# Grouped-query attention: the third converted block moves into its own job, and V is scaled instead of checked

## The chip, the cores and the metric

The kernel runs on one core of a Trainium2 chip. The metric is the device time of one execution in microseconds (us). Engines: PE (TensorE, matrix products), ACT (ScalarE, exponentials), DVE (VectorE, element by element), POOL (GpSimd, likewise, and issue of DMAs), SP (issue of DMAs). Each takes its instructions in order; they wait for each other by semaphores.

## The reference

```python
batch, seq, n_heads, n_kv_heads, dim = 8, 512, 32, 8, 64
scores = np.einsum('bhqd,bhkd->bhqk', Q, K_expanded) * (1 / np.sqrt(dim))
weights = np.exp(scores - np.max(scores, axis=-1, keepdims=True))
weights = weights / (np.sum(weights, axis=-1, keepdims=True) + 1e-10)
output = np.einsum('bhqk,bhkd->bhqd', weights, V_expanded)
```

Q, K and V are float32, four query heads share one head of K and V. The output is float32.

## The kernel before, in words

The maximum is not subtracted. The sums of the exponentials come out of the second product by a column of ones beside V, and each output is multiplied by the reciprocal of its sum. The sums (and V's largest value) are checked against bounds on the chip; where a bound is broken, a general path computes the result anew after the fast one.

Work is cut into 64 jobs, one for each batch and head of K: four query heads, in two pairs (`NPAIR`), of 512 queries against 512 keys. Scores are computed transposed, keys on partitions: a block is 128 keys by 512 queries, and a job has 16 of them: pair i, key chunk kc, head m of the pair. Two blocks that differ in m use different halves of PE's rows and are written next to each other as one pair of 128x1024. In `act_tile` PE writes such a pair to an `s_ps` tile of PSUM (two of these, two banks each) and ACT turns it into exponentials `pt` in 16 bits.

Not all blocks go to ACT. The first blocks of pair 1 are converted by DVE and POOL through bits of a 16-bit number: DVE scales the scores into an integer `u` (`exp_d`, L313); it masks its low bits, `f` (L325); POOL makes a factor `g` (L330) and a product `w` (L336); DVE adds `u` and `w` into `pt` one job later (`exp_d4`, L349). A narrow job takes two blocks so (jobs 0 to 3, those with j % 5 equal to 2, and the last two). A wide job (`WIDE`) takes three, which leaves ACT six pairs and one half, 128x512. The scores that DVE reads stand in `d_ps`, one tile of two banks, which also receives the transposed queries.

In a wide job j of before, the order by engine is: four ACT pairs, with the scores of DVE's first two blocks (`exp_d(j, 0, 2, ...)`) after the first; two groups of 16 products of the job before (`pv`, L377) between them; its reciprocal and scaling (`norm`, L417 and L422), which free the one pv tile; then a new `d_ps` tile whose second bank takes the score of ACT's lone half (`beside`), while the queries of job j + 2 are transposed into its first bank (L215). `apart` declares for ACT's reading and the transposes and copy that they touch different banks of the tile, since the recording layer otherwise orders users of one tile. DVE adds the previous job's `w` (L349), masks its own `u` (L325) and copies the queries (L220). In the last wide job of a round of five, the factor `g` is made on DVE after this copy. Next, the third block of job j + 1 is written alone to the second bank (`exp_d(j + 1, 2, 3, ...)`) and converted by DVE (L313, 128x512). The remaining two ACT pairs and 32 pv matmuls lie between.

V arrives by POOL's DMA queue and is converted to bf16 by it, straight into the tile `vt` with 65 columns for each head, the last of them ones. `check_v` reduces each quarter of it to its largest absolute value (L238); `check_sums` compares 128 reciprocals at a time with two bounds (L388).

The order is written by hand (`manual_schedule`); the recording layer adds the waits.

Of the kernel before, what the change touches and what calls it, by code (L numbers as in the profile page):

```python
# [33 lines left out]
SUM_LO = 64.0  # L34
SUM_HI = 57344.0
V_HI = 1.0e15
NLAST = 16
LAST_SUMS = NLAST * 2 * 4


WIDE = lambda j: 4 <= j < 62 and j % 5 != 2


# [24 lines left out]
def fast_path(ctx, tc, Q, K, V, out, flag, ident):  # L68
# [13 lines left out]
    const_pool = ctx.enter_context(tc.tile_pool(name="const", bufs=1))  # L82
    qnat_pool = ctx.enter_context(tc.tile_pool(name="qnat", bufs=4))
    knat_pool = ctx.enter_context(tc.tile_pool(name="knat", bufs=2))
    qt_pool = ctx.enter_context(tc.tile_pool(name="qt", bufs=3))
# [10 lines left out]

    ok = const_pool.tile([128, SPB * 2 * SC], FP32, name="ok")
    okv = const_pool.tile([128, B * SC], FP32, name="okv")
    okall = const_pool.tile([128, 1], FP32, name="okall")
# [4 lines left out]
    vt = [const_pool.tile([128, SC, KV, D + 1], BF16, name=f"v{j}") for j in range(2)]  # L104
# [4 lines left out]
    kn, qn, kt, qt, twice = {}, {}, {}, {}, {}  # L109

# [8 lines left out]

    def load_v(b, lo=0):  # L120
        to = vt[b % 2][:, :, lo:, 0:D]
        of = V[b, :, lo:, :].rearrange("(p sc) g d -> p sc g d", p=128)
        if lo:
            for sc in range(SC):
                nc.gpsimd.dma_start(out=to[:, sc], in_=of[:, sc])
        else:
            nc.gpsimd.dma_start(  # L127
                out=to.rearrange("p sc g d -> p (sc g) d"),
                in_=of.rearrange("p sc g d -> p (sc g) d"),
            )  # L130

# [103 lines left out]

    def check_v(b, sc):
        n = b * SC + sc
        nc.vector.tensor_reduce(  # L238
            out=okv[:, n:n + 1], in_=vt[b % 2][:, sc, :, 0:D], op=ALU.max, axis=AX.XY,
            apply_absolute_value=True,  # L240
        )

    NJOB = NU * 2
    DPAIR = NPAIR - 1

    def taken(j):
        return 3 if WIDE(j) else 2

# [3 lines left out]
    def act_tiles(j):  # L252
# [7 lines left out]

    CHECKS = {
        (j, at): divmod(n, SC) for n, (j, at) in enumerate(
            [(j, 0) for j in (3, 4, 6, 7, 8, 11, 12, 16, 17, 21, 22, 23, 26, 27, 31, 32)]
            + [(j, 0) for j in (36, 37, 38, 41, 42, 46, 47, 48, 51, 52, 56, 57, 60, 61, 62)]
            + [(62, 1)]
        )
    }

    KEYS = dict(zip((4, 10, 16, 26, 36, 41, 50), range(1, B)))
# [5 lines left out]
    LOADS = {1: [(load_q, 1, 0, 2 * HPG), (load_q, 1, 2 * HPG, 4 * HPG)]}  # L275
    in_jobs(load_k, 1, [3, 8, 12, 23, 32, 38, 48])
    in_jobs(load_q, 2, [3, 7, 8, 12, 17, 22, 23, 27, 32, 37, 38, 42, 47, 48])
    in_jobs(load_v, 1, [4, 13, 18, 28, 33, 43, 53])

# [15 lines left out]

    def act_tile(j, n, spare=None):
        group = act_tiles(j)[n]
        i, kc, lo = group[0]
        ps = s_pool.tile([128, 2, S], FP32, name="s_ps") if spare is None else spare
        for _, _, m in group:  # L300
            scores(j, ps[:, m, :], i, kc, m)
        return nc.scalar.activation(  # L302
            out=jobs[j]["pt"][:, i, kc, lo:, :], in_=ps[:, lo:, :], func=EXP, scale=scale
        )

    def exp_d(j, lo, hi, ps, other=None):
        st = jobs.setdefault(j, {})
        if "u" not in st:
            for name, dtype in (("u", I16), ("f", I16), ("g", BF16), ("w", BF16)):
                st[name] = dve_pool.tile([128, 3, S], dtype, name=name + "16")[:, 0:taken(j), :]  # L310
        for n in range(lo, hi):
            apart(scores(j, ps[:, n - lo, :], DPAIR, *divmod(d_block(j) + n, 2)), other)
        return lambda: nc.vector.tensor_scalar(  # L313
            out=st["u"][:, lo:hi, :], in0=ps[:, 0:hi - lo, :], scalar1=A_U, scalar2=B_U,
            op0=ALU.mult, op1=ALU.add,
        )

    def exp_d2(j, engine=None):  # L320
        st = jobs[j]
        by_bits = engine is None
        engine = engine or nc.gpsimd
        odd = j == NJOB - 2 or WIDE(j) and not WIDE(j + 1)
        nc.vector.tensor_single_scalar(  # L325
            out=st["f"], in_=st["u"], scalar=1023, op=ALU.bitwise_and
        )

        def factor():
            (nc.vector if odd else engine).tensor_scalar(  # L330
                out=st["g"], in0=st["f"], scalar1=-EXP_F1,
                scalar2=EXP_K * 2.0 ** (24 * by_bits), op0=ALU.add, op1=ALU.mult,
            )

        def product():
            engine.tensor_tensor(  # L336
                out=st["w"], in0=st["g"], in1=st["f"].bitcast(FP16) if by_bits else st["f"],
                op=ALU.mult,
            )
# [25 lines left out]
    def pv(j, i, lo, hi):  # L365
# [9 lines left out]
        for n in range(lo, hi):  # L375
# [3 lines left out]
                st["pt"][:, i, kc, m, qc * 128:(qc + 1) * 128],  # L379
                vt[b % 2][:, kc, 2 * gp + g, :],  # L380
# [4 lines left out]
    def in_bounds(outs, inv, first):  # L385
        ops = ((1.0 / SUM_HI, ALU.is_ge), (1.0 / SUM_LO, ALU.is_le))
        for out_, in1, (bound, op) in zip(outs, (first, outs[0]), ops):
            nc.vector.scalar_tensor_tensor(  # L388
                out=out_, in0=inv, scalar=bound, in1=in1, op0=op, op1=ALU.mult
            )  # L390


    full = []

    def check_sums():
        while full:
            flat = invs.pop(full.pop()).rearrange("p s m qc -> p (s m qc)")
            in_bounds((ok, ok), flat, ok)

    inv_last = const_pool.tile([128, NLAST, 2, SC], FP32, name="inv_last")  # L400

    def norm(j, i):
# [31 lines left out]
        if left > NLAST and n == SPB - 1:  # L434
            full.append(k)

    def all_checks():
        assert not full and not invs
        vmax = const_pool.tile([128, 1], FP32, name="vmax")
        nc.vector.tensor_reduce(out=vmax, in_=okv, op=ALU.max, axis=AX.X)  # L440
        okmin = const_pool.tile([128, 1], FP32, name="okmin")
        nc.vector.tensor_reduce(out=okmin, in_=ok, op=ALU.min, axis=AX.X)
        nc.gpsimd.tensor_scalar(
            out=okall, in0=vmax, scalar1=V_HI, scalar2=okmin, op0=ALU.is_le, op1=ALU.mult
        )

    LIMITS = ((1.0 / SUM_HI, ALU.is_ge), (1.0 / SUM_LO, ALU.is_le))
    rights = [const_pool.tile([128, LAST_SUMS], BF16, name=f"right{n}") for n in range(2)]

    def last_rights(lo, hi, first=None):  # L450
        inv = inv_last.rearrange("p s m qc -> p (s m qc)")
        for engine, right, (bound, op) in zip((first or nc.gpsimd, nc.gpsimd), rights, LIMITS):
            engine.tensor_scalar(
                out=right[:, lo:hi], in0=inv[:, lo:hi],
                scalar1=bound, scalar2=okall, op0=op, op1=ALU.mult,
            )
# [39 lines left out]
    for j in range(2):  # L496
        nc.gpsimd.memset(vt[j][:, :, :, D:D + 1], 1.0)
    load_k(0, 2, 4)
    load_k(0, 4, KV)
    load_q(0, 8, 16)  # L500
    load_v_head(0, 1)
    load_v(0, 2)
    nc.gpsimd.memset(ones, 1.0)
    nc.gpsimd.memset(ok, 1.0)

# [51 lines left out]
    two_keys(1)  # L557
    exp_d(0, 0, 2, d_tile())()
    act_tile(0, 3)
# [10 lines left out]
    for j in range(1, NJOB - 1):  # L570
# [8 lines left out]
        if j == 1:  # L579
            dma_k(0, 2)  # L580
        if j in KEYS:
# [6 lines left out]
        exp_d(j, 0, 2, d_tile())()  # L588
# [12 lines left out]
        bank = d_tile()  # L601
        beside = act_tile(j, 4, bank) if taken(j) > 2 else None

# [7 lines left out]
        rest = exp_d2(j)  # L611
        copies = [read() for read in reads]
        if rest:
            rest()
        if taken(j) == 2:
            act_tile(j, 4)
        pv(last, 1, 0, cut[0])
        act_tile(j, 5)
        if beside:
# [3 lines left out]
        if (j, 1) in CHECKS:  # L623
            check_v(*CHECKS[j, 1])
        if not beside:
            pv(last, 1, *cut)
        act_tile(j, 6)
        pv(last, 1, cut[1], 32)
# [5 lines left out]
    act_tile(j, 0)  # L634
    exp_d(j, 0, 2, d_tile())()
    all_checks()
# [139 lines left out]
```

## Time and profile before

| | |
|---|---|
| median of three runs | 404.75 us (404.59 to 404.81) |
| profiled execution, its own time | 404.57 us |
| its span in the profile | 402.8 us |
| busy share PE, DVE, ACT, POOL | 93%, 91%, 98%, 71% |
| ACT exponentials of 128x1024 | 400, 1122 ns each in the record |
| ACT exponentials of 128x512 from d_ps | 47, 724 ns each |
| DVE conversions of 128x512 | 47, 684 ns each |
| V checks | 32, 676 ns each |

The span runs from the first to the last recorded instruction; 1.8 us of the execution's time lie around it. A group's row gives line, engine, operation, output and input tiles, count, then busy time and mean length of one, then the idle time of the engine just before and what ended it. Lengths on ACT overlap: the next one starts before the last one's end, so the distance of ends gives the pace. In a timeline a row starts with its start and length in us; rows of equal instructions that follow each other are one row with a count.

### The profile page before, as it was taken

How to read it: one execution, taken by the hardware profiler on the slowest of the kernel's cores; microseconds unless marked ns; L12 is line 12 of the kernel's file. 1: busy time of each engine (PE TensorE's matmuls, PEld its weight loads, DVE VectorE, ACT ScalarE, POOL GpSimd, SP SyncE). 2: the span in 40 equal slices, each digit the busy share in tenths (PEclk: the TensorE clock that was granted, in tenths of full speed). 3: DMA queues.
4: the chain of work that ended last, by engine and by line, in shares of the span. 5: the costliest groups of instructions: out<-in, count | busy, mean ns of one | idle time of the engine just before them, and what ended most of it. 6: DMA issues, size and time to landing. Idle time of an engine off the chain costs nothing.

```text
span 402.8 us, 12997 instructions
## 1 busy us (share of the span) xinstructions
PE 375.8 (93%) x5670; PEld 228.0 (57%) x5670; DVE 366.4 (91%) x635; ACT 393.9 (98%) x454; POOL 286.8 (71%) x169
## 2 busy tenths in 40 slices
PE   7999999999999999999999999999999999999985
PEld 3565555555555555555555555555555555556554
DVE  4788998999999999999999999999999999999996
ACT  5999999999999999999999999999999999999995
POOL 9848577597587687687687686677776767765752
PEclk9999999999999999999999999999999999999999
DMA  9979999899999259999259999679369959222206
GB/s 145 163 190 182 91 288 225 164 211 237 184 214 206 107 88 247 192 239 182 107 84 226 168 227 197 208 109 252 110 170 202 175 169 128 107 106 106 88 34 201
DMA packets 82893, 67.73 MB, mean 168 GB/s; under 512 B 52752, under 2 KB 57872, under 8 KB 82832
## 3 DMA queue, kind: packets, MB, share of 16 engines
q0 software_dynamic: 45072, 24.91, 48.3%
q1 hardware_dynamic: 36688, 41.49, 36.6%
q8 instruction: 45, 0.74, 0.7%
q10 hardware_dynamic: 1072, 0.46, 0.4%
q14 instruction: 16, 0.13, 0.1%
HBM read 50.33 MB, written 33.55 MB: 208 GB/s over the span
## 4 chain that ended last, share of the span: by engine, by line
ACT 29%; PE 25%; POOL 24%; DVE 20%; issue 2%; ACTq 0%; DVEq 0%
ACT pt L302 28%; POOL w L336 16%; PE pv L377 12%; PE s_ps L284 9%; POOL g L330 8%; DVE pt L349 8%; DVE o_sb L422 4%; DVE f L325 4%; DVE qt L220 2%; PE d_ps L215 2%; DVE g L330 1%; DVE inv L417 1%; PE d_ps L284 1%; PE s_ps L510 1%; PE d_ps L377 0%
## 5 line engine op out<-in xcount | busy, mean ns | idle before, releaser
L302 ACT ACTIVATE pt<-s_ps 128x1024 f16<-128x1024 f32 x400 | 379.0, 1122 | 0.3 <-PE s_ps L284 0.2
L336 POOL TENSOR_TENSOR w<-g,f 128x1536 bf16<-128x1536 bf16 (+1 forms) x63 | 179.6, 2851 | 37.6 <-DVE g L330 33.4
L377 PEld LDWEIGHTS <-pt 128*128 128x128 f16 x4096 | 142.1, 98 | 81.2 <-issue 41.6
L377 PE MATMUL pv<-v,pt 128*128 128x65 bf16 x4032 | 177.8, 195 | 3.7 <-DVE o_sb L422 2.2
L284 PE MATMUL s_ps<-qt,kt 64*128 64x512 bf16 x746 | 152.3, 384 | 12.0 <-ACT pt L302 10.0
L330 POOL TENSOR_SCALAR g<-f 128x1536 bf16<-128x1536 int16 (+1 forms) x50 | 67.1, 1341 | 69.1 <-DVE f L325 69.0
L313 DVE TENSOR_SCALAR u<-d_ps 128x1024 int16<-128x1024 f32 (+1 forms) x111 | 109.9, 990 | 0.3
L284 PEld LDWEIGHTS <-kt 64*128 64x128 bf16 x960 | 50.2, 93 | 55.3 <-issue 31.5
L422 DVE TENSOR_TENSOR o_sb<-pv,inv 128x512 f32<-128x512 f32 x112 | 77.5, 692 | 3.9
L284 PE MATMUL d_ps<-qt,kt 64*128 64x512 bf16 x214 | 58.4, 376 | 3.5 <-ACT pt L302 0.3
L349 DVE TENSOR_TENSOR pt<-u,w 128x1536 uint16<-128x1536 int16 (+1 forms) x64 | 56.4, 882 | 2.3 <-POOL w L336 0.2
L220 DVE COPY qt<-d_ps 128x1024 bf16<-128x1024 bf16 x62 | 42.3, 684 | 0.0
L215 PEld LDWEIGHTS <-q_nat 128*128 128x128 bf16 x508 | 28.5, 98 | 23.8 <-issue 23.8
L417 DVE RECIPROCAL inv<-pv 128x8 f32<-128x8 f32 x112 | 23.1, 207 | 17.4 <-PE pv L377 16.0
L215 PE MATMUL d_ps<-ident,q_nat 128*128 128x128 bf16 x496 | 38.3, 220 | 0.0
L302 ACT ACTIVATE pt<-d_ps 128x512 f16<-128x512 f32 x47 | 34.0, 724 | 0.0
L325 DVE TENSOR_SCALAR f<-u 128x1536 int16<-128x1536 int16 (+1 forms) x64 | 33.3, 521 | 0.0
L238 DVE TENSOR_REDUCE okv<-v 128x1 f32<-128x512 bf16 x32 | 21.6, 676 | 0.0
L142 POOL DMA_DIRECT2D q_nat<-in_Q_dram x19 | 15.2, 801 | 0.1
L284 PE MATMUL s_ps<-qt,kt_first 64*128 64x512 bf16 x56 | 11.1, 396 | 1.9 <-ACT pt L302 1.5
L127 POOL DMA_DIRECT2D v<-in_V_dram x7 | 12.3, 1753 | 0.0
L422 DVE TENSOR_TENSOR o_sb<-pv,inv_last 128x512 f32<-128x512 f32 x14 | 9.7, 692 | 0.5
(61 smaller groups left out, 62.7 us busy)
## 6 DMA issues: line engine op xcount, KB each, us to landing
out_dram<-o_sb SPq DMA_DIRECT2D x31, 1024.0 KB, 6.1
q_nat<-in_Q_dram POOLq DMA_DIRECT2D x14, 1024.0 KB, 12.4
k_nat<-in_K_dram POOLq DMA_DIRECT2D x7, 512.0 KB, 7.5
v<-in_V_dram POOLq DMA_DIRECT2D x7, 512.0 KB, 13.6
kt<-kt SPq DMA_DIRECT2D x14, 256.0 KB, 4.0
q_nat<-in_Q_dram POOLq DMA_DIRECT2D x3, 512.0 KB, 7.5
out_dram<-o_sb SPq DMA_DIRECT2D x3, 256.0 KB, 2.4
kt<-k_nat SPq DMA_TRANSPOSE x32, 5.9
```

What stands on the lines that cost most here:

```text
L215: nc.tensor.transpose(ps[:, i, sc, :], qn[u // 2][:, sc, h:h + 2, :], ident),
L220: return done, lambda: apart(nc.vector.tensor_copy(out=qt[u][:, g, lo:hi, :], in_=ps[:, lo:hi, :, :].rearrange("p i sc c -> p i (sc c)")), ...
L284: return nc.tensor.matmul(ps, keys[64 * m:64 * m + 64, g if u == 0 else g ^ m, kc * 128:(kc + 1) * 128], qt[u][64 * m:64 * m + 64, g, i, : ...
L302: return nc.scalar.activation(out=jobs[j]["pt"][:, i, kc, lo:, :], in_=ps[:, lo:, :], func=EXP, scale=scale)
L313: return lambda: nc.vector.tensor_scalar(out=st["u"][:, lo:hi, :], in0=ps[:, 0:hi - lo, :], scalar1=A_U, scalar2=B_U, op0=ALU.mult, op1=AL ...
L325: nc.vector.tensor_single_scalar(out=st["f"], in_=st["u"], scalar=1023, op=ALU.bitwise_and)
L330: (nc.vector if odd else engine).tensor_scalar(out=st["g"], in0=st["f"], scalar1=-EXP_F1, scalar2=EXP_K * 2.0 ** (24 * by_bits), op0=ALU.a ...
L336: engine.tensor_tensor(out=st["w"], in0=st["g"], in1=st["f"].bitcast(FP16) if by_bits else st["f"], op=ALU.mult,)
L349: nc.vector.tensor_tensor(out=st["pt"][:, DPAIR, :, :, :].rearrange("p kc m q -> p (kc m) q")[:, d_block(j):d_block(j) + n, :].bitcast(U16 ...
L377: nc.tensor.matmul(st["pv"][i][:, m, qc, :], st["pt"][:, i, kc, m, qc * 128:(qc + 1) * 128], vt[b % 2][:, kc, 2 * gp + g, :], start=(n < 2 ...
L417: nc.vector.reciprocal(out=inv, in_=sums[:, :, :, D:D + 1])
L422: nc.vector.tensor_tensor(out=osb[u][:, :, h:h + 2, :].rearrange("p qc m d -> p m qc d"), in0=sums[:, :, :, 0:D], in1=inv[:, :, :, None].t ...
```

## The change

Three things change together.

The third block of a wide job is no longer prepared one job ahead. In its own job, `odd_tile` writes two blocks as a pair to one `d_ps` tile: ACT reads the second bank (its lone half) and DVE converts the first (`to_bits`). The two pairs of ACT that follow, and twelve pv matmuls, come before the query transposes, which then overwrite the first bank; 20 pv matmuls follow the transposes. On DVE the conversion stands ahead of `exp_d4`, the masking and the query copy.

V is loaded as it is into a tile of its own, in long runs (`v_nat`), and DVE multiplies it by 2 to the power of -16 into `vt`, whose heads now stand 72 columns apart; the column of ones holds the same factor, so the quotient is unchanged. V of the first batch is still loaded into `vt` and scaled there by POOL in three parts. The check of V's values is gone.

The check of the sums keeps the smallest, the largest and the sum of each 128 reciprocals with three reductions and compares them at the end.

```diff
+V_UNIT = 2.0 ** -16
+V_STEP = 72
...
-    def load_v(b, lo=0):
...
+    def load_v(b):
+        vn[b] = vnat_pool.tile([128, SC, KV, D], BF16, name="v_nat")
+        nc.gpsimd.dma_start(
+            out=vn[b], in_=V[b].rearrange("(p sc) g d -> p sc g d", p=128)
+        )
...
+    def units_v(b, lo=0, hi=KV):
+        to = vt[b % 2][:, :, lo:hi, 0:D]
+        if b:
+            nc.vector.tensor_single_scalar(out=to, in_=vn.pop(b), scalar=V_UNIT, op=ALU.mult)
         else:
+            nc.gpsimd.tensor_single_scalar(out=to, in_=to, scalar=V_UNIT, op=ALU.mult)
...
-    def check_v(b, sc):
...
+    SUMS = (11, 21, 26, 36, 41, 51, 61)
+    UNITS = dict(zip((8, 13, 23, 28, 38, 43, 53), range(1, B)))
...
+    def odd_tile(j, ps):
+        (i, kc, m), = act_tiles(j)[4]
+        scores(j, ps[:, 0, :], i, kc, 0)
+        scores(j, ps[:, m, :], i, kc, m)
+        st = jobs[j]
+        left = nc.scalar.activation(
+            out=st["pt"][:, i, kc, m:, :], in_=ps[:, m:, :], func=EXP, scale=scale
+        )
+        to_bits(st["u"][:, 2:3, :], ps[:, 0:1, :])
+        return left
+
+    def to_bits(out, in_):
+        nc.vector.tensor_scalar(
+            out=out, in0=in_, scalar1=A_U, scalar2=B_U, op0=ALU.mult, op1=ALU.add
+        )
...
-            in_bounds((ok, ok), flat, ok)
+        for n, op in enumerate((ALU.min, ALU.max, ALU.add)):
+            nc.vector.tensor_reduce(out=found[:, n, k:k + 1], in_=flat, op=op, axis=AX.X)
...
-        cut = (11, 19) if taken(j) < 3 else (4, 18) if taken(last) < 3 else (4, 16)
+        cut = (12, 12) if taken(j) > 2 else (11, 19)
...
-        if j % 5 == 3:
+        if j in SUMS:
             check_sums()
-        if (j, 0) in CHECKS:
-            check_v(*CHECKS[j, 0])
+        if j in UNITS:
+            units_v(UNITS[j])
+            if UNITS[j] + 1 < B:
+                load_v(UNITS[j] + 1)
...
-        beside = act_tile(j, 4, bank) if taken(j) > 2 else None
+        beside = None
+        if taken(j) > 2:
+            beside = odd_tile(j, bank)
+            act_tile(j, 5)
+            pv(last, 1, 0, cut[0])
+            act_tile(j, 6)
...
-        if taken(j + 1) > 2:
-            exp_d(j + 1, 2, taken(j + 1), bank[:, 1:2, :], copies[0])()
```

More of the change, by code (lines that the diff above doesn't have):

```diff
@@ L41 @@
 WIDE = lambda j: 4 <= j < 62 and j % 5 != 2
+ALONE = lambda j: j == 62 or WIDE(j) and not WIDE(j + 1)
 @with_exitstack
@@ L95, in fast_path @@
     pv_pool = ctx.enter_context(tc.tile_pool(name="pv", bufs=1, space=PS))
-    ok = const_pool.tile([128, SPB * 2 * SC], FP32, name="ok")
-    okv = const_pool.tile([128, B * SC], FP32, name="okv")
-    okall = const_pool.tile([128, 1], FP32, name="okall")
+    found = const_pool.tile([128, 3, B - 1], FP32, name="found")
+    seen_all = const_pool.tile([128, 3], FP32, name="seen_all")
+    okall = const_pool.tile([128, 3], FP32, name="okall")
     gate = const_pool.tile([1, 1], FP16, name="gate")
@@ L103, in fast_path @@
     kt_first = const_pool.tile([128, 2, 2, S], BF16, name="kt_first")
-    vt = [const_pool.tile([128, SC, KV, D + 1], BF16, name=f"v{j}") for j in range(2)]
+    vt = [const_pool.tile([128, SC, KV, V_STEP], BF16, name=f"v{j}") for j in range(2)]
     kf = [const_pool.tile([128, SC, D], FP32, name=f"kf{g}") for g in range(2)]
     qf = const_pool.tile([128, SC, 2, D], FP32, name="qf")
-    kn, qn, kt, qt, twice = {}, {}, {}, {}, {}
+    kn, vn, qn, kt, qt, twice = {}, {}, {}, {}, {}, {}
     def load_k(b, lo=0, hi=KV):
@@ L117, in load_k, with first_v @@
         )
-    def load_v(b, lo=0):
[L121 to L125, printed above, removed]
-        else:
[L127 to L130, printed above, removed]
+    def load_v(b):
[3 more added lines that the diff above has]
+        )
+    def first_v(lo):
+        of = V[0, :, lo:, :].rearrange("(p sc) g d -> p sc g d", p=128)
+        for sc in range(SC):
+            nc.gpsimd.dma_start(out=vt[0][:, sc, lo:, 0:D], in_=of[:, sc])
+    def units_v(b, lo=0, hi=KV):
+        to = vt[b % 2][:, :, lo:hi, 0:D]
+        if b:
+            nc.vector.tensor_single_scalar(out=to, in_=vn.pop(b), scalar=V_UNIT, op=ALU.mult)
+        else:
+            nc.gpsimd.tensor_single_scalar(out=to, in_=to, scalar=V_UNIT, op=ALU.mult)
     def load_v_head(b, g):
@@ L234, in piece @@
         pieces.append((bank, done, copy))
-    def check_v(b, sc):
[L237 to L241, printed above, removed]
     NJOB = NU * 2
@@ L294, in open_job, with act_tile @@
         jobs.setdefault(j, {}).update(pt=pt, pv={})
-    def act_tile(j, n, spare=None):
+    def act_tile(j, n):
         group = act_tiles(j)[n]
         i, kc, lo = group[0]
-        ps = s_pool.tile([128, 2, S], FP32, name="s_ps") if spare is None else spare
+        ps = s_tile()
         for _, _, m in group:
@@ L304, in act_tile, with exp_d @@
         )
[L306 to L315, printed above, removed]
-        )
+    def odd_tile(j, ps):
[5 more added lines that the diff above has]
+            out=st["pt"][:, i, kc, m:, :], in_=ps[:, m:, :], func=EXP, scale=scale
+        )
+        to_bits(st["u"][:, 2:3, :], ps[:, 0:1, :])
[4 more added lines that the diff above has]
+        )
+    def exp_d(j, ps):
+        st = jobs[j]
+        for name, dtype in (("u", I16), ("f", I16), ("g", BF16), ("w", BF16)):
+            st[name] = dve_pool.tile([128, 3, S], dtype, name=name + "16")[:, 0:taken(j), :]
+        for n in range(2):
+            scores(j, ps[:, n, :], DPAIR, *divmod(d_block(j) + n, 2))
+        to_bits(st["u"][:, 0:2, :], ps)
     def exp_d2(j, engine=None):
@@ L323, in exp_d2 @@
         engine = engine or nc.gpsimd
-        odd = j == NJOB - 2 or WIDE(j) and not WIDE(j + 1)
+        odd = ALONE(j)
         nc.vector.tensor_single_scalar(
@@ L383, in pv @@
             )
[L385 to L390, printed above, removed]
     full = []
     def check_sums():
-        while full:
-            flat = invs.pop(full.pop()).rearrange("p s m qc -> p (s m qc)")
-            in_bounds((ok, ok), flat, ok)
+        k = full.pop()
+        flat = invs.pop(k).rearrange("p s m qc -> p (s m qc)")
+        for n, op in enumerate((ALU.min, ALU.max, ALU.add)):
+            nc.vector.tensor_reduce(out=found[:, n, k:k + 1], in_=flat, op=op, axis=AX.X)
     inv_last = const_pool.tile([128, NLAST, 2, SC], FP32, name="inv_last")
@@ L435, in norm @@
             full.append(k)
+    LEAST, MOST = 1.0 / SUM_HI / V_UNIT, 1.0 / SUM_LO / V_UNIT
     def all_checks():
         assert not full and not invs
[L439 to L447, printed above, removed]
+        for n, op in enumerate((ALU.min, ALU.max, ALU.add)):
+            nc.vector.tensor_reduce(out=seen_all[:, n:n + 1], in_=found[:, n, :], op=op, axis=AX.X)
+        right = 1.0
+        for n, (bound, op) in enumerate(((LEAST, ALU.is_ge), (MOST, ALU.is_le), (1.0e30, ALU.is_le))):
+            nc.gpsimd.tensor_scalar(
+                out=okall[:, n:n + 1], in0=seen_all[:, n:n + 1],
+                scalar1=bound, scalar2=right, op0=op, op1=ALU.mult,
+            )
+            right = okall[:, n:n + 1]
+    LIMITS = ((LEAST, ALU.is_ge), (MOST, ALU.is_le))
     rights = [const_pool.tile([128, LAST_SUMS], BF16, name=f"right{n}") for n in range(2)]
@@ L454, in last_rights @@
                 out=right[:, lo:hi], in0=inv[:, lo:hi],
-                scalar1=bound, scalar2=okall, op0=op, op1=ALU.mult,
+                scalar1=bound, scalar2=okall[:, 2:3], op0=op, op1=ALU.mult,
             )
@@ L501, in fast_path @@
     load_v_head(0, 1)
-    load_v(0, 2)
+    first_v(2)
     nc.gpsimd.memset(ones, 1.0)
-    nc.gpsimd.memset(ok, 1.0)
+    units_v(0, 0, 1)
     def keep_busy(*columns, at=None):
@@ L580, in fast_path @@
             dma_k(0, 2)
+            units_v(0, 1, 2)
+        if j == 2:
+            units_v(0, 2)
         if j in KEYS:
             dma_k(KEYS[j])
-        cut = (11, 19) if taken(j) < 3 else (4, 18) if taken(last) < 3 else (4, 16)
+        cut = (12, 12) if taken(j) > 2 else (11, 19)
         act_tile(j, 0)
@@ L611, in fast_path @@
         rest = exp_d2(j)
-        copies = [read() for read in reads]
+        for read in reads:
+            read()
         if rest:
             rest()
-        if taken(j) == 2:
+        if not beside:
             act_tile(j, 4)
-        pv(last, 1, 0, cut[0])
-        act_tile(j, 5)
-        if beside:
+            pv(last, 1, 0, cut[0])
+            act_tile(j, 5)
             pv(last, 1, *cut)
-        if taken(j + 1) > 2:
-            exp_d(j + 1, 2, taken(j + 1), bank[:, 1:2, :], copies[0])()
[L623 to L627, printed above, removed]
+            act_tile(j, 6)
         pv(last, 1, cut[1], 32)
```

25 lines of the change are left out of this document (9 added, 16 removed).

## The prediction

> **What bounds the kernel now.** I read the page's busy shares first, then its groups, then the timeline of two neighbouring jobs in the middle. The first three rows are the page's share of the span and its two groups of exponentials.
>
> ```profile
> span 402.8 us, 12997 instructions
> PE 375.8 (93%) x5670; PEld 228.0 (57%) x5670; DVE 366.4 (91%) x635; ACT 393.9 (98%) x454; POOL 286.8 (71%) x169
> ...
> L302 ACT ACTIVATE pt<-s_ps 128x1024 f16<-128x1024 f32 x400 | 379.0, 1122 | 0.3 <-PE s_ps L284 0.2
> ...
> L302 ACT ACTIVATE pt<-d_ps 128x512 f16<-128x512 f32 x47 | 34.0, 724 | 0.0
> ```
>
> ACT stands still for 0.3 us before 447 exponentials: it sets the pace. PE and DVE are close behind it, so what they are made to wait for matters. The timeline (start, length, engine, operation) of wide job 30 and the beginning of job 31:
>
> ```profile
> 189.10 4.82 ACT L302 ACTIVATE pt<-s_ps 128x1024 f16<-128x1024 f32 x5
> ...
> 192.42 0.38 PE L284 MATMUL d_ps<-qt,kt 64*128 64x512 bf16 x1
> 192.54 0.69 DVE L422 TENSOR_TENSOR o_sb<-pv,inv 128x512 f32<-128x512 f32 x1
> 192.73 0.62 PE L215 MATMUL d_ps<-ident,q_nat 128*128 128x128 bf16 x8
> 193.29 0.96 DVE L349 TENSOR_TENSOR pt<-u,w 128x1536 uint16<-128x1536 int16 x1
> 193.69 0.72 ACT L302 ACTIVATE pt<-d_ps 128x512 f16<-128x512 f32 x1
> 194.17 0.55 DVE L325 TENSOR_SCALAR f<-u 128x1536 int16<-128x1536 int16 x1
> 194.17 5.75 ACT L302 ACTIVATE pt<-s_ps 128x1024 f16<-128x1024 f32 x6
> 194.46 0.37 PE L284 MATMUL d_ps<-qt,kt 64*128 64x512 bf16 x1
> 194.64 0.68 DVE L220 COPY qt<-d_ps 128x1024 bf16<-128x1024 bf16 x1
> 194.81 1.47 POOL L330 TENSOR_SCALAR g<-f 128x1536 bf16<-128x1536 int16 x1 [1.55 <-DVE f L325]
> 195.24 0.68 DVE L313 TENSOR_SCALAR u<-d_ps 128x512 int16<-128x512 f32 x1
> 195.84 0.20 DVE L417 RECIPROCAL inv<-pv 128x8 f32<-128x8 f32 x1
> 196.07 0.69 DVE L422 TENSOR_TENSOR o_sb<-pv,inv 128x512 f32<-128x512 f32 x1
> 196.37 3.10 POOL L336 TENSOR_TENSOR w<-g,f 128x1536 bf16<-128x1536 bf16 x1
> 196.82 0.66 PE L377 MATMUL pv<-v,pt 128*128 128x65 bf16 x16
> 197.41 0.39 PE L284 MATMUL s_ps<-qt,kt 64*128 64x512 bf16 x2
> 199.50 0.96 DVE L349 TENSOR_TENSOR pt<-u,w 128x1536 uint16<-128x1536 int16 x1
> 199.70 0.71 ACT L302 ACTIVATE pt<-d_ps 128x512 f16<-128x512 f32 x1
> 201.44 0.55 DVE L330 TENSOR_SCALAR g<-f 128x1536 bf16<-128x1536 int16 x1
> ```
>
> ACT's ends give its true pace. The half tile ends at 194.41, the six whole tiles after it at 199.92: 5.51 / 6 = 0.918 us each. The previous whole tile ended at 193.92, so a half tile costs 0.49. A wide job is 6 x 0.918 + 0.49 = 6.00 us, and 400 x 0.918 + 47 x 0.49 is 390 us, nearly the whole span. What can be won between the first exponential and the last is under 2 us; what can be lost is any wait that reaches ACT.
>
> Where a wait reaches it: ACT works through two score tiles, so PE may refill one only when ACT has ended the tile two before. Whatever holds PE or, through PE's in-order queue, DVE for over some tenths of a microsecond is ACT's loss.
>
> **The change part by part.**
>
> The third block. Before, its scores were a lone matmul (194.46) in the job ahead, behind ACT's half tile, and DVE converted it last (195.24), after the query copy. Now both halves of one d_ps tile are written as a pair in the same job; ACT exponentiates one half, DVE converts the other. 47 lone matmuls go; one held PE from 192.42 to 192.73, 0.31 us, so some 14.6 us of PE work, none of it ACT's time (idle 0.3). Worth nothing by itself.
>
> The wait that it adds. In the built program DVE's conversion of the half (to_bits, 128x512) carries one wait: on ACT's half tile of the same job. The two read different halves, but nothing declares them apart, so the tile layer orders the two readers. DVE is in order, and this conversion now stands ahead of the 3-block sum (L349), the masking (L325), the query copy (L220), on the last job of a round the factor (L330), and the reciprocal and scaling (L417, L422) that free the pv tile. The eight query transposes on PE also wait for it, because they overwrite its half, and behind them in PE's queue stand 20 pv matmuls and the next job's scores.
>
> The ring that follows, counted from the end of ACT's half tile in job j, with distances from start to next start in the rows above: wait passed on 0.05 (194.41 to 194.46); conversion 0.60 (195.24 to 195.84); sum 0.88 (193.29 to 194.17); masking 0.47 (to 194.64); copy 0.60 (to 195.24); reciprocal 0.23 (to 196.07); scaling 0.69 to its end; passed to PE 0.06 (196.76 to 196.82); 16 pv matmuls 0.59 (to 197.41); the third score pair of job j+1 0.39; passed to ACT 0.05, as above. That is 4.61 us until ACT may start the third tile of job j+1. A first tile after a stand takes about 1.02, the shortest of its group:
>
> ```profile
> L302 ACT ACTIVATE pt<-s_ps x400: 1018/1122/1339, 7.0 to 396.6; 128x1024 f16<-128x1024 f32 x134
> ```
>
> So that tile ends 5.63 after the half tile. Unhindered, it ends five whole tiles after it, 5 x 0.918 = 4.59. Loss: 1.04 us, in each wide job.
>
> A second path gives nearly the same and so confirms it: conversion ended 0.05 + 0.68 = 0.73, transposes 0.05 + 0.56 (192.73 to 193.29) to 1.34; the sum ends at 0.05 + 0.60 + 0.96 = 1.61, its 16 pv matmuls run 1.66 to 2.25, the next job's first scores and hop 0.44, tile 1.02: 3.71 against 3 x 0.918 = 2.75, a loss of 0.96. The two don't add; the longer counts.
>
> Three kinds of wide job. Of each round the first follows a narrow job, whose sum covers 1024 columns and is shorter; the last has the factor on DVE between copy and reciprocal.
>
> ```profile
> L349 DVE TENSOR_TENSOR pt<-u,w 128x1536 uint16<-128x1536 int16 x47 | 44.8, 954 | 2.2 <-POOL w L336 0.2
> L349 DVE TENSOR_TENSOR pt<-u,w 128x1024 uint16<-128x1024 int16 x17 | 11.6, 682 | 0.1
> L325 DVE TENSOR_SCALAR f<-u 128x1536 int16<-128x1536 int16 x47 | 26.0, 554 | 0.0
> L325 DVE TENSOR_SCALAR f<-u 128x1024 int16<-128x1024 int16 x17 | 7.3, 430 | 0.0
> L238 DVE TENSOR_REDUCE okv<-v 128x1 f32<-128x512 bf16 x32 | 21.6, 676 | 0.0
> L330 DVE TENSOR_SCALAR g<-f 128x1536 bf16<-128x1536 int16 x12 | 6.6, 551 | 0.0
> L388 DVE SCALAR_TENSOR_TENSOR ok<-inv,ok 128x128 f32<-128x128 f32 x14 | 4.6, 332 | 0.2
> L442 DVE TENSOR_REDUCE okmin<-ok 128x1 f32<-128x128 f32 x1 | 0.3, 277 | 0.0
> L127 POOL DMA_DIRECT2D v<-in_V_dram x7 | 12.3, 1753 | 0.0
> L114 POOL DMA_DIRECT2D k_nat<-in_K_dram x9 | 5.7, 632 | 0.0
> L453 POOL TENSOR_SCALAR right<-inv_last,okall 128x112 bf16<-128x112 f32 x2 | 1.4, 680 | 3.5 <-DVE inv_last L417 3.4
> ```
>
> And of the page's list of DMA issues:
>
> ```profile
> v<-in_V_dram POOLq DMA_DIRECT2D x7, 512.0 KB, 13.6
> ```
>
> First of a round (12): 1.04 - (0.95 - 0.68) = 0.77. Last (12): the factor adds 0.47 (201.44 to the reciprocal at 201.91, by its length less the usual overlap of 0.08): 1.51. The other 23: 1.04. Sum 9.2 + 18.1 + 23.9 = 51.2 us. The factor and product on POOL (1.47 + 3.10) still end before the next sum, since the job is longer now; a narrow job adds no wait of this kind.
>
> V checks gone. 32 reductions of 676 ns, 21.6 us of DVE. They stood between the pair's conversion and the first reciprocal of a job, where DVE waits for PE anyway; now it waits for ACT later in the job too. Gain on the path: 0.
>
> Scaling V. Seven DVE operations of 2048 columns in the same place. Fast, as the masking goes from 1024 to 1536 (0.124 per 512): 0.430 + 0.248 = 0.68, hidden as the check was. Slow, as the conversions from PSUM go (1215 and 684 ns for 1024 and 512): 0.684 + 3 x 0.531 = 2.28, up to 1.6 late each, 11 us in all. I take the fast end, 16-bit in and out as the masking. On POOL, three scalings of 256, 256 and 1536 columns at the start: at most 1.47 each (its 1536 row), in gaps of POOL before its factors; 0, and if that cover were gone about 2 us.
>
> Sum checks. Three reductions (277 ns or less each) instead of two of 332, now in last jobs of a round: 0.8 us ahead of the reciprocal, and DVE then stands over 1 us for ACT; 0. Without that cover 7 x 0.2. At the end, three reductions and three small POOL operations for two and one: POOL idles 3.4 us before the first operation that needs them, so 0; without that cover under 1 us.
>
> V in long packets. Seven issues of 1753 ns on POOL become shorter (K loads take 632 on the mean); POOL is not on the ring. V landed 13.6 us after its issue and is now issued four jobs (24 us) or more before its scaling: 0. If not, the 12.3 us of issue bounds it on either side.
>
> Total 404.57 + 51.2 = 455.8 against the profiled execution's own 404.57 us (span 402.8 and 1.8 around it); the median is 404.75, so I say 456.
>
> **A rule weighed.** The rows show ACT and DVE reading PSUM at the same time in different tiles (DVE's conversion at 195.24 inside ACT's six tiles). The Trainium skill, "PSUM — Partial Sum Buffer", section "PSUM bank collisions raise a hardware error", says the same for any two different banks: only one bank shared by two engines collides. By that rule the two halves here, two banks, could be read side by side and the time would be that of the first rival; the trace agrees with the rule, but an order put into the program holds whatever the memory allows.
>
> **Rivals.**
>
> (1) Not slower: the two readers overlap, the wait costs nothing. Place: to_bits of the half. DVE is free at 192.54 + 0.69 = 193.23 and the scores are there at 192.80, so the conversion could start 1.23 us before the 194.46 that the wait allows; the ring is only 1.04 too long, so from 1.04 earlier on nothing reaches ACT. Time 404 to 404.6; ACT has 0.3 us to give back. For it: the skill's rule above. Against: the wait stands in the program.
>
> (2) The ring is shorter than its terms, because PE and DVE hand over faster when both are drained, or ACT's depth of two tiles absorbs more: 0.7 of the sum, 36 us, 440. For it: the rows come from crowded queues. Against: two paths give 0.96 and 1.04.
>
> (3) V is scaled slowly: 2.28 us seven times, and it delays the first reciprocal and the pv tile: 456 + 11 = 467. For it: rows of 65 or 72 columns are not whole runs. Against: 16-bit from and to SBUF.
>
> **Chances.** Forecast (448 to 462) 0.73, (1) 0.06, (2) 0.12, (3) 0.09. The range takes in (2) and (3): 438 to 468; it leaves out (1) and what lies beyond. A difference under 0.2% (0.8 us) can't be told from no change: faster 0.02, same 0.04, slower 0.94.
>
> **What would show it.** ACT's group of whole tiles no longer busy throughout: some 50 us of idle, before the first or third tile of a job, released by PE's scores. The half's conversion waits on ACT, starting right after ACT's half tile ends, 47 times. The chain of waits passes through ACT's half tile, DVE's conversion, sum, masking, copy, scaling, and PE, job after job; POOL falls off it. A wide job lasts about 7.0 us instead of 6.0. DVE's V scaling near 0.7 us. The forecast is wrong if ACT still runs 30 of 30 us in mid-kernel, or if the conversion starts before ACT's half tile has ended.

## The result and the profile after

The changed kernel takes 455.76 us (median of four runs, 455.68 to 456.85) against 404.73: 1.127 times, 95% interval 1.125 to 1.129. The forecast was 456. Medians and ratios leave out executions over 1.5% above the fastest of their kernel; only two were such, both of the tenth kernel below.

The page of the changed kernel: its span, its busy shares, the chain of waits by engine, and the groups that answer to those of before.

```profile
span 455.1 us, 12933 instructions
PE 369.9 (81%) x5670; PEld 228.0 (50%) x5670; DVE 355.7 (78%) x618; ACT 401.5 (88%) x454; POOL 285.4 (63%) x173
...
ACT 54%; DVE 23%; PE 15%; issue 7%; ACTq 0%; DVEq 0%
...
L300 ACT ACTIVATE pt<-s_ps 128x1024 f16<-128x1024 f32 x400 | 381.7, 1042 | 45.0 <-ACT pt L300 36.3
...
L317 DVE TENSOR_SCALAR u<-d_ps 128x1024 int16<-128x1024 f32 (+1 forms) x111 | 110.3, 993 | 48.5 <-ACT pt L310 48.5
```

ACT stood still for 0.3 us before its whole tiles; now it is 45.0. DVE's conversions (L317), before which DVE stood 0.3 us in all, now wait 48.5 us for ACT's half tile. POOL, 24% of the chain of waits before, has left it. Two rows of the waits (who waited for whom, us in total, times, longest) give the count, and show the query transposes on PE (L226) waiting 36.8 us for that conversion:

```profile
DVE u L317 <- ACT pt L310: 48.5, 47, 1.3
...
PE d_ps L226 <- DVE u L317: 36.8, 47, 0.8
```

47 times each: once in each wide job. The ring, first in the timeline of DVE alone in job 30 and the turn to job 31, then in rows of PE for the same turn, then in the timeline of ACT alone in jobs 30, 31 and the narrow job 32:

```profile
218.53 0.69 DVE L317 TENSOR_SCALAR u<-d_ps 128x512 int16<-128x512 f32 x1 [0.94 <-ACT pt L310]
219.14 0.95 DVE L358 TENSOR_TENSOR pt<-u,w 128x1536 uint16<-128x1536 int16 x1
220.00 0.55 DVE L334 TENSOR_SCALAR f<-u 128x1536 int16<-128x1536 int16 x1
220.47 0.68 DVE L231 COPY qt<-d_ps 128x1024 bf16<-128x1024 bf16 x1
221.07 0.20 DVE L419 RECIPROCAL inv<-pv 128x8 f32<-128x8 f32 x1
221.31 0.69 DVE L424 TENSOR_TENSOR o_sb<-pv,inv 128x512 f32<-128x512 f32 x1
```

```profile
219.28 0.61 PE L226 MATMUL d_ps<-ident,q_nat 128*128 128x128 bf16 x8 [0.77 <-DVE u L317]
...
219.72 1.08 PE L386 MATMUL pv<-v,pt 128*128 128x65 bf16 x20
...
220.14 0.54 PEld L386 LDWEIGHTS <-pt 128*128 128x128 f16 x16 [0.26 <-DVE pt L358]
...
220.74 0.39 PE L282 MATMUL s_ps<-qt,kt 64*128 64x512 bf16 x2
```

```profile
217.90 0.59 ACT L310 ACTIVATE pt<-d_ps 128x512 f16<-128x512 f32 x1
218.38 1.95 ACT L300 ACTIVATE pt<-s_ps 128x1024 f16<-128x1024 f32 x2
221.22 3.80 ACT L300 ACTIVATE pt<-s_ps 128x1024 f16<-128x1024 f32 x4 [0.89 <-ACT pt L300]
224.92 0.59 ACT L310 ACTIVATE pt<-d_ps 128x512 f16<-128x512 f32 x1
225.39 1.95 ACT L300 ACTIVATE pt<-s_ps 128x1024 f16<-128x1024 f32 x2
228.23 1.94 ACT L300 ACTIVATE pt<-s_ps 128x1024 f16<-128x1024 f32 x2 [0.88 <-ACT pt L300]
230.56 1.02 ACT L300 ACTIVATE pt<-s_ps 128x1024 f16<-128x1024 f32 x1 [0.39 <-PE s_ps L282]
```

ACT's half tile ends at 218.49, DVE's conversion starts at 218.53 after 0.94 us idle, though DVE was free of its previous work at 217.59. From half tile to half tile it is 224.92 - 217.90 = 7.02 us, where before it was 199.70 - 193.69 = 6.01. On PE the transposes wait for the conversion, 16 of the 20 products behind them (their weights are loaded by PEld) for DVE's sum, and the next job's first scores end at 220.74 + 0.39 = 221.13. ACT starts on them at 221.22. The profile puts this stand of ACT down to ACT itself, as 36.3 of the 45.0 us; but in 44 of the 47 turns ACT starts 0.09 us after these scores have ended. In the narrow job 32 ACT stands twice, for its first tile and for its third.

### The profile page after: what moved, and what is told of

It is laid out like the page before. It is cut to its first block, busy times and chain, and to the rows that moved or that the text cites. A ratio compares the mean times of both kernels' runs of the same rounds, so it can differ in the third digit from the quotient of the medians.

```text
span 455.1 us, 12933 instructions
## 1 busy us (share of the span) xinstructions
PE 369.9 (81%) x5670; PEld 228.0 (50%) x5670; DVE 355.7 (78%) x618; ACT 401.5 (88%) x454; POOL 285.4 (63%) x173
## 4 chain that ended last, share of the span: by engine, by line
ACT 54%; DVE 23%; PE 15%; issue 7%; ACTq 0%; DVEq 0%
ACT pt L300 49%; DVE u L317 7%; DVE pt L358 7%; PE pv L386 6%; ACT pt L310 5%; PE s_ps L282 5%; DVE f L334 3%; DVE o_sb L424 2%; PE d_ps L226 2%; DVE qt L231 2%; DVE g L339 1%; PE s_ps L516 1%; DVE inv L419 0%; PE s_ps L386 0%; PE d_ps L386 0%
## 5 line engine op out<-in xcount | busy, mean ns | idle before, releaser
L300 ACT ACTIVATE pt<-s_ps 128x1024 f16<-128x1024 f32 x400 | 381.7, 1042 | 45.0 <-ACT pt L300 36.3
L386 PE MATMUL pv<-v,pt 128*128 128x65 bf16 x4032 | 175.5, 194 | 25.7 <-DVE o_sb L424 16.7
L386 PEld LDWEIGHTS <-pt 128*128 128x128 f16 x4096 | 143.6, 98 | 95.6 <-DVE o_sb L424 62.5
L282 PE MATMUL s_ps<-qt,kt 64*128 64x512 bf16 x746 | 145.9, 383 | 10.0 <-ACT pt L300 8.3
L317 DVE TENSOR_SCALAR u<-d_ps 128x1024 int16<-128x1024 f32 (+1 forms) x111 | 110.3, 993 | 48.5 <-ACT pt L310 48.5
L282 PEld LDWEIGHTS <-kt 64*128 64x128 bf16 x960 | 47.1, 93 | 65.8 <-issue 43.5
L226 PE MATMUL d_ps<-ident,q_nat 128*128 128x128 bf16 x496 | 37.8, 219 | 36.8 <-DVE u L317 36.8
L226 PEld LDWEIGHTS <-q_nat 128*128 128x128 bf16 x508 | 32.2, 97 | 50.4 <-issue 50.4
L282 PE MATMUL d_ps<-qt,kt 64*128 64x512 bf16 x214 | 41.4, 377 | 4.5
L310 ACT ACTIVATE pt<-d_ps 128x512 f16<-128x512 f32 x47 | 29.1, 618 | 0.0
L282 PE MATMUL s_ps<-qt,kt_first 64*128 64x512 bf16 x56 | 11.6, 415 | 2.1 <-ACT pt L300 2.0
L339 DVE TENSOR_SCALAR g<-f 128x1536 bf16<-128x1536 int16 (+1 forms) x14 | 7.5, 533 | 0.1
L127 POOL DMA_DIRECT2D v_nat<-in_V_dram x7 | 4.2, 602 | 5.1 <-DVE inv L419 5.1
```

The lines of the kernel that those rows point to most:

```text
L226: nc.tensor.transpose(ps[:, i, sc, :], qn[u // 2][:, sc, h:h + 2, :], ident),
L282: return nc.tensor.matmul(ps, keys[64 * m:64 * m + 64, g if u == 0 else g ^ m, kc * 128:(kc + 1) * 128], qt[u][64 * m:64 * m + 64, g, i, : ...
L300: return nc.scalar.activation(out=jobs[j]["pt"][:, i, kc, lo:, :], in_=ps[:, lo:, :], func=EXP, scale=scale)
L310: left = nc.scalar.activation(out=st["pt"][:, i, kc, m:, :], in_=ps[:, m:, :], func=EXP, scale=scale)
L317: nc.vector.tensor_scalar(out=out, in0=in_, scalar1=A_U, scalar2=B_U, op0=ALU.mult, op1=ALU.add)
L339: (nc.vector if odd else engine).tensor_scalar(out=st["g"], in0=st["f"], scalar1=-EXP_F1, scalar2=EXP_K * 2.0 ** (24 * by_bits), op0=ALU.a ...
```

## Experiments

Times of kernels that ran once are told without an interval; ratios are to the kernel before on the same chip. Where a loss by job is given, it is the distance between the ends of ACT's tiles less 0.917 us for a whole tile and 0.49 for a half, from the profile of that run.

**1. The wait taken away.** The two readers of the tile are declared apart; they read different banks.

```diff
-        to_bits(st["u"][:, 2:3, :], ps[:, 0:1, :])
+        apart(to_bits(st["u"][:, 2:3, :], ps[:, 0:1, :]), left)
```

> Edit: DVE's conversion of the half and ACT's reading of the other half are declared apart (two banks of one tile); nothing else. Theory (the wait on ACT makes the ring): the conversion starts up to 1.2 us earlier, the whole loss of wide jobs goes, 404 to 410 us; a few tenths may stay in each narrow job after a last wide job, where DVE now has the conversion (0.60) and the factor (0.47) in one job: 12 x up to 0.4 = 4 us. Rival (the new places of the conversion, the transposes and the 20 products cost the time, wait or not): 430 us or more. Rival (scaling V and its loads): no change from 455.8.

Measured: 412.7 us, ratio 1.020 (1.017 to 1.022). 43 of 51 us are gone; the wait made them. The new places of the instructions stayed, so they explain at most the 8 us that are left. Jobs 31 and 32 of its timeline:

```profile
203.09 0.68 DVE L317 TENSOR_SCALAR u<-d_ps 128x512 int16<-128x512 f32 x1
...
203.49 0.73 ACT L310 ACTIVATE pt<-d_ps 128x512 f16<-128x512 f32 x1
...
203.90 0.96 DVE L358 TENSOR_TENSOR pt<-u,w 128x1536 uint16<-128x1536 int16 x1
...
206.55 0.69 DVE L424 TENSOR_TENSOR o_sb<-pv,inv 128x512 f32<-128x512 f32 x1
...
207.30 0.66 PE L386 MATMUL pv<-v,pt 128*128 128x65 bf16 x16 [0.70 <-DVE o_sb L424]
...
208.32 2.86 ACT L300 ACTIVATE pt<-s_ps 128x1024 f16<-128x1024 f32 x3 [0.39 <-PE s_ps L282]
```

The conversion now starts 0.4 us before ACT's half tile and both read at once, each at its usual length. Wide jobs lose next to nothing. What is left, 8.5 us in the profile (0.8 in that of the kernel before), lies in the 13 narrow jobs (6.3 us, 0.55 in most) and in the first jobs (1.7). In the narrow job PE's products wait 0.70 us for the scaling that frees the pv tile. DVE's sum starts 0.81 us after the conversion did, where the ring had 0.60: POOL's product, which it needs, ends only 0.03 us ahead of it (it ran from 200.78 for 3.09).

**2 and 3. The wait kept in 12 jobs only**: in the last wide job of each round, then in the first.

```diff
-        apart(to_bits(st["u"][:, 2:3, :], ps[:, 0:1, :]), left)
+        kept = ALONE(j)            # third run: not WIDE(j - 1)
+        apart(to_bits(st["u"][:, 2:3, :], ps[:, 0:1, :]), None if kept else left)
```

> Edit: as the one that declares the two apart, but in the last wide job of each round (12 of them) the wait stays. Theory: each wait costs its own price whatever the other jobs do; the last jobs lost 1.48 us each in the profile of the changed kernel, so 12 x 1.48 = 17.8 us over the kernel without any wait, less what that one already loses in those narrow jobs (up to 4): 14 to 18 over it. Rival (the loss needs the chain from job to job): well under 10 over it.

> Edit: as the one that declares the two apart, but in the first wide job of each round (12) the wait stays. Theory: 12 x 0.75 = 9.0 us over the kernel without any wait, up to 12 if the delay carries into the next wide jobs, which have little spare time on DVE. Rival (the loss needs the chain from job to job): under 4 over it.

Measured, once each: 423.6 us with the wait in last jobs, 427.45 in first jobs, 10.9 and 14.8 above the kernel without it; both lie outside what was expected (14 to 18, and 9 to 12). In the first of the two profiles each narrow job loses 1.49 us, as in the changed kernel; without the wait most had lost 0.55 already, so 0.94 is added, 11.6 in all 12. The price belongs to the job and needs no chain; what it replaces was larger than the 4 us I allowed. With the wait in first jobs, the next job loses 0.75 as before, and the two jobs behind it 0.2 each, which they don't without it. Rows of that profile, two sums on DVE and POOL's product between them:

```profile
199.12 0.96 DVE L359 TENSOR_TENSOR pt<-u,w 128x1536 uint16<-128x1536 int16 x1
...
202.20 3.10 POOL L346 TENSOR_TENSOR w<-g,f 128x1536 bf16<-128x1536 bf16 x1
...
205.33 0.96 DVE L359 TENSOR_TENSOR pt<-u,w 128x1536 uint16<-128x1536 int16 x1
```

Sum, masking, factor, product and again the sum take 205.33 - 199.12 = 6.21 us, 0.2 more than ACT's 6.00, since each sum starts as soon as the product is there. The kernel before has the same turn in job 30 (199.50 - 193.29) without a loss: it is made up for by the narrow job 32, whose product is there 1.35 us before its sum. The delay of the first job seems to use up that slack, and then every further turn costs ACT its 0.2. So the sum of the prices holds where all jobs wait, and a single wait costs more or less than its own, by its neighbours.

**4. The sum ahead of the conversion**, in the changed kernel with its wait.

```diff
-            beside = odd_tile(j, bank)
+            beside, half = odd_tile(j, bank)
+            exp_d4(last)
+            half()
...
-        exp_d4(last)
+        if not beside:
+            exp_d4(last)
```

> Edit: the changed kernel with its wait, but on DVE the sum (three blocks, 0.88 us) stands ahead of the half's conversion, so it leaves the ring. Theory with DVE's ring alone: the loss falls by 0.88 to about 0.16 a job and 0.63 in last jobs, 405 + 35 x 0.16 + 12 x 0.63 = 418 us. Theory with the second path as well (PE's transposes wait for the conversion; 20 products and the next job's first scores stand behind them; the sum is no longer in it): 0.05 + 0.68 + 0.05 + 1.14 + 0.44 + 1.02 = 3.4 us against 2.75, a loss of about 0.7 in each of 47 jobs, 438 us. The two paths are told apart by 20 us.

Measured, once: 449.8 us. Both expectations missed: not 418, and 12 above 438. The first job of a round came out as the path over PE said: the job behind it loses 0.68 (0.75 in the changed kernel), so that path is real. Nearly all other wide jobs make the job behind them lose 0.93 or more, by a third ring. Its timeline, of DVE alone and then of POOL alone:

```profile
214.69 0.96 DVE L357 TENSOR_TENSOR pt<-u,w 128x1536 uint16<-128x1536 int16 x1 [0.53 <-POOL w L344]
215.56 0.68 DVE L316 TENSOR_SCALAR u<-d_ps 128x512 int16<-128x512 f32 x1
216.28 0.56 DVE L333 TENSOR_SCALAR f<-u 128x1536 int16<-128x1536 int16 x1
...
221.62 0.96 DVE L357 TENSOR_TENSOR pt<-u,w 128x1536 uint16<-128x1536 int16 x1 [0.53 <-POOL w L344]
```

```profile
216.93 1.47 POOL L338 TENSOR_SCALAR g<-f 128x1536 bf16<-128x1536 int16 x1 [2.28 <-DVE f L333]
218.49 3.10 POOL L344 TENSOR_TENSOR w<-g,f 128x1536 bf16<-128x1536 bf16 x1
```

Sum, conversion, masking, factor, product and again the sum: 221.62 - 214.69 = 6.93 us for one turn, longer than ACT's 6.00. It is the turn of 6.21 us above, made longer by the conversion between sum and masking, and POOL's product comes too late for the next sum. In the changed kernel the conversion stands ahead of the sum, outside this turn, and a turn there lasts 7.0 us anyway.

**5, 6 and 7. V apart from the third block.** The fifth kernel is the first one without POOL's scalings (the unit is 1, the calls are taken out); the sixth has only the V part and the sum checks, with the third block as before; the seventh only the third block.

```diff
-V_UNIT = 2.0 ** -16
+V_UNIT = 1.0
...
-    units_v(0, 0, 1)
...
-            units_v(0, 1, 2)
-        if j == 2:
-            units_v(0, 2)
```

> Edit: as the one that declares the two apart, and V is taken as it is in the first batch (the unit of V is 1 throughout, so POOL's three scalings go; the seven on DVE stay, by 1). What it leaves out: the scaling of V. Theory: POOL's scaling of 1536 columns took 4.08 us and held DVE's sum beside it (2.42 instead of 0.68 us), which cost ACT some 0.7 us in job 2; so 0.5 to 1.0 us less than the kernel that only declares the two apart. Rival (the delay in jobs 2 and 3 of the profile came from the lower granted clock there alone): no difference.

> Edit: the kernel before with V's loads, scaling and sum checks of the changed one; the third block is handled as before. Theory: V costs only what POOL's first scaling costs, 0 to 1 us over the kernel before, 404.7 to 405.8. Rival (V's scaling on DVE, 0.92 us where 0.68 was taken, or its loads, cost ACT time in mid-kernel): 408 or more.

> Edit: the kernel before with only the third block's new place (V and the checks of V and sums as before; one V check of job 62 stands in job 58). Theory: the ring makes all of the loss, 404.7 + 50.5 = 455, up to 4 more if V checks of 0.68 us don't fit where DVE stands 0.54 us for PE. Rival (V makes a good part): 440 or less.

Measured: 410.2 (ratio 1.014, 1.012 to 1.016), 410.45 (1.015, 1.013 to 1.017; executions between 406.6 and 412.1) and 455.4 (1.126, 1.124 to 1.128). The third block alone makes the whole loss. But V alone costs 6 us, where I expected at most one; in the kernel without the wait it costs 2.5 (0.5 to 1.0 expected), and beside the wait it can't be told from nothing. It starts in job 2. POOL and DVE in the profile of the changed kernel, and the granted clock in two stretches (length, busy time and count of PE, PEld, DVE, ACT and POOL, then the clock as a share of full speed, and two figures on DMA):

```profile
20.82 4.08 POOL L141 TENSOR_SCALAR v<-v 128x1536 bf16<-128x1536 bf16 x1
...
22.14 2.42 DVE L358 TENSOR_TENSOR pt<-u,w 128x1024 uint16<-128x1024 int16 x1
```

```profile
26.00:28.00 2.00, 1.52 (x20) 0.83 (x18) 1.97 (x4) 1.60 (x2) 1.92 (x2) 0.81 0.00 0
28.00:30.00 2.00, 2.00 (x27) 1.30 (x24) 0.42 (x2) 1.36 (x2) 1.84 (x3) 0.50 0.93 349
```

POOL's scaling takes 4.08 us, and DVE's sum beside it 2.42 instead of 0.68. In all seven profiles with this scaling the sum is so long, 2.42 to 2.97, and ends 0.33 us before POOL does, although it starts 0.78 to 1.32 after POOL: DVE is held until POOL has nearly finished. The masking and the query copy behind it come late, and PE stands. In this profile and the sixth kernel's, PE's granted clock then falls to 0.50 for about 3 us, and ACT loses 2.1 and 2.3 us in job 3; in the other five the clock stays at 1.00 there, and ACT loses 0.9 to 1.3.

**8. V without POOL's scaling**, the third block as before.

> Edit: the kernel before with V's loads, the seven operations on DVE and the sum checks of the changed one, but the unit of V is 1 and POOL scales nothing. What it leaves out: the scaling of V. Theory (the 6 us that V costs alone come from POOL's scaling of 1536 columns in job 2, which holds DVE's sum, then PE, then lowers the granted clock for some us): the time of the kernel before, 404.0 to 405.0. Rival (V's operations of 0.92 us on DVE or its loads cost the time in mid-kernel): 408 or more.

Measured: 404.14 us, ratio 0.9994 (0.9985 to 1.0003), no difference from the kernel before. So the long loads, the seven operations on DVE (0.80 us each here, 0.92 in the changed kernel) and the sum checks cost nothing; what V costs comes with POOL's scalings, of which the traces show the one in job 2 at work. That kernel leaves the unit of V out.

**9. The factor behind the freeing of the pv tile**, on the fifth kernel.

```diff
-        if rest:
+        if rest and not beside:
             rest()
+            rest = None
...
         norm(last, 1)
+        if rest:
+            rest()
```

> Edit: the kernel without the wait and without the scaling of V in the first batch; in last wide jobs the factor on DVE moves from before the reciprocal and scaling that free the pv tile to behind them. What it leaves out: the scaling of V. Theory (the 0.5 us left in each of 12 narrow jobs is the factor's 0.47 ahead of the freeing of the pv tile): 6 us less than without the move, 404 to 405; if the product on POOL, now 0.8 later, delays the narrow job's sum, up to 0.3 of each 0.5 stays, 407. Rival (the conversion's new place itself): no change from 410.2.

Measured: 416.1 us, ratio 1.029 (1.027 to 1.030): worse by 6, where 6 less was expected. The rows of its job 32, POOL's product and the sum that needs it:

```profile
208.81 3.09 POOL L345 TENSOR_TENSOR w<-g,f 128x1536 bf16<-128x1536 bf16 x1 [3.45 <-DVE g L339]
...
211.93 0.96 DVE L358 TENSOR_TENSOR pt<-u,w 128x1536 uint16<-128x1536 int16 x1 [1.07 <-POOL w L345]
```

The third tile of the narrow job no longer waits for the pv tile, but the sum waits 1.07 us for POOL, and PE's products behind it. So it was the factor that cost 0.5 us at the third tile, but neither of the two places tried for its 0.47 on DVE is free.

**10 and 11. What V costs alone, once more.** The tenth kernel is the sixth again, for another profile. In the eleventh DVE scales the first batch's 1536 columns.

```diff
-            nc.gpsimd.tensor_single_scalar(out=to, in_=to, scalar=V_UNIT, op=ALU.mult)
+            (nc.vector if lo == 2 else nc.gpsimd).tensor_single_scalar(
+                out=to, in_=to, scalar=V_UNIT, op=ALU.mult
+            )
```

> The kernel with the V part alone, profiled a second time. Its timed executions took 410 to 412 us at granted clocks of 0.989 to 0.994, the profiled one 406.6 with 2.6 us lost in jobs 2 and 3. Theory (the lowered granted clock after the stand in job 2 costs the rest): a profile near 410 us shows the loss in the first jobs, spread over more jobs at a clock of 0.5. Rival (it is lost elsewhere): losses in mid-kernel at full clock.

> Edit: the kernel with the V part alone, but the first batch's 1536 columns of V are scaled by DVE in job 2, not by POOL; the two pieces of 256 columns stay on POOL. Nothing is left out. Theory (POOL's 4.08 us and what it holds up are the whole cost of V): 404.0 to 405.0, as the kernel before. Rival (any scaling at that place stops PE long enough): 407 or more.

Measured: the tenth 405.1 to 411.1 us in five executions, ratio 1.008 (1.006 to 1.011), so that V alone costs 3 to 6 us by the two runs; the eleventh 406.0, ratio 1.005 (1.003 to 1.006), where 404 to 405 was expected. DVE's operation took 2.50 us there, beside POOL's product, and ended 0.41 after it; the seven larger ones took 0.80 on the mean. Job 2 lost 1.5 us: cheaper than on POOL, but not nothing. No other job lost more than before, so the unit itself costs nothing. The tenth kernel's profiled execution, of 411.1 us, refutes my account of the spread. It lost 1.0 in job 3, but 6.0 in jobs 8 to 10, 4.6 of them in job 9. There:

```profile
70.13 0.69 DVE L413 TENSOR_TENSOR o_sb<-pv,inv 128x512 f32<-128x512 f32 x1 [3.93 <-DMA out_dram<-o_sb]
...
71.86 1.02 ACT L300 ACTIVATE pt<-s_ps 128x1024 f16<-128x1024 f32 x1 [3.71 <-PE s_ps L282]
```

The scaling of an output waits 3.93 us for an earlier store to land, which frees the tile that it writes (three are in use); only then does the clock fall. Nor is a lower clock needed for a loss: one of the five executions took 407.5 us at a granted clock of 1.00. That store was issued at 53.95, 0.37 us behind POOL's next load of K, and landed 16.1 us later; in the profiles of the sixth, eighth and eleventh kernels it was issued 0.56 to 0.73 us ahead of that load and landed after 9.7 to 10.4. Whether this order makes it late was not tried, and how the delay in job 2 could bring it about stays open.

## Why the prediction was right

**The wait and its ring.** Right as to the wait and its size, job by job: forecast 1.04, 0.77 and 1.51 us for a middle, a first and a last wide job; measured 1.03, 0.77 and 1.49 on the mean (23, 12 and 12 jobs), together 50.7 us against 51.2. For the middle job it can be read above: 7.02 - 6.01 = 1.01. For the last one, ACT's half tile ends at 225.51 and the third tile of job 32 at 230.56 + 1.02 = 231.58, which is 6.07 instead of 4.59. The first experiment shows that the wait is the cause, the seventh that nothing else is needed.

**Which path binds.** Here the forecast had it the wrong way round. I took the ring over DVE (1.04) as the one that counts and the path over PE (0.96) as its check. In middle jobs ACT loses 0.99 at the first tile of the next job, by the path over PE (conversion, sum, products, first scores), and only 0.03 more at the third, by DVE's ring; the profile's chain of waits takes in neither copy nor scaling in the turn shown above. The total came out although the order of the paths did not: it was luck that they lie within 0.08 us of each other. In last jobs the factor adds 0.5 at the third tile, as forecast.

**What was worth nothing.** The V checks, the sum checks, the long loads and the seven scalings on DVE were rightly costed at 0, as the eighth experiment shows; a scaling took 0.92 us where I took 0.68, and it was covered. The lone matmuls were not tried apart. POOL's scaling was mis-sized: I bounded it by the factor's 1.47 us for 1536 columns, "in gaps of POOL", and it took 4.08 and held up DVE. In the changed kernel's profile the first four jobs lose 2.5 us where they lost 0.4, so the 2 us that I gave for a missing cover was the right size there; alone it costs 3 to 6.

**The rival that the two readers overlap.** Once declared apart, the two do read at once: the first experiment's trace has the conversion from 203.09 to 203.77 and ACT's half tile from 203.49. The Trainium skill's "PSUM — Partial Sum Buffer" ("PSUM bank collisions raise a hardware error") says the same of two different banks. The time of that rival was wrong all the same: 404 to 404.6 was forecast, 410.2 is what is left without wait and scaling. I compared the 1.23 us with the 1.04 of a middle job, not with the 1.51 of a last one; the difference of 0.28 showed as 0.5 in most narrow jobs, and the 0.21 by which POOL's product holds back the sum there makes up the rest.

**The rival that V is scaled slowly** on DVE didn't come about (0.92 us, not 2.28), nor the shorter ring (50.7 us, not 36).

## What to carry to other kernels

When two engines read two halves of one tile, look at the waits of the built program: the layer that records them may order the readers, and an operation at the head of an in-order queue then carries that wait to everything behind it. Price it as a ring, from the end of the awaited operation back to the next one of its kind, and by every path, since two or three may be nearly equal and taking one step out only hands the bound to the next. Work removed from other engines gained nothing here, since ACT had no idle time; the spare tenths of its neighbours are what a moved operation uses up. A ring can also be longer than the bottleneck's pace for a few jobs and make up for it in a lighter one, as POOL's turn of 6.21 us does in the kernel before; a delay that uses up this slack then costs more than its own length, as the third experiment suggests.

## What was not expected

POOL's scaling of 1536 bf16 columns in place, 64 of every 72, took 4.08 us, where its factor over 1536 contiguous columns takes 1.47; DVE's sum beside it took 2.42 to 2.97 us in seven profiles instead of 0.68, and always ended 0.33 us before POOL. On DVE the same operation took 2.50 us beside POOL's product, though the larger ones took 0.80. And in one execution a store waited for in job 9 cost more than the delay in job 2; that the one caused the other is not shown.

No version was found that beats the kernel before: by the distances of its ends, ACT there has 0.8 us to give back between the first exponential and the last, and the best of the others, 404.14 us, can't be told from it (ratio 0.9985 to 1.0003).
